# Gated linear attention on one core: chunks of 64 tokens joined in pairs

## The chip, the cores and the metric

The kernel runs on one core of a Trainium2 chip. The metric is device time of one execution in microseconds (us); less is better. The core's engines work side by side, each on its own queue in order: TensorE (PE: products; PEld is its loading of weights), VectorE (DVE), ScalarE (ACT), GpSimd (POOL) and SyncE (SP, which here issues nearly all transfers). TensorE multiplies a stationary operand, of up to 128 rows (the contraction) by 128 columns, with a moving one of up to 512 columns, and adds up in banks of PSUM; all else lies in SBUF.

## The reference

A model of four layers on 256 tokens with 2048 channels: RWKV-7, gated linear attention (GLA), SSD, RWKV-7 again. Each layer norms x, shifts and scales it by vectors made from a condition c with the large matrices `ada_w`, mixes tokens, projects out and adds to x. All numbers are float32. The change concerns the GLA layer: 4 heads, 256 key channels and 512 value channels a head, chunks of C = 64 tokens:

```python
qc = chunks(q * DK ** -0.5, DK); kc = chunks(k, DK); vc = chunks(v, DV)
bcum = jnp.cumsum(chunks(log_alpha, DK), axis=-2)          # log decay, summed within the chunk
b_ref = bcum[..., C // 2 - 1:C // 2, :]
scores = jnp.einsum('nbhik,nbhjk->nbhij', qc * jnp.exp(bcum - b_ref), kc * jnp.exp(b_ref - bcum))
o_intra = jnp.einsum('nbhij,nbhjv->nbhiv', jnp.where(causal, scores, 0.0), vc)
b_last = bcum[..., -1:, :]
q_from_start = qc * jnp.exp(bcum)
k_to_end = kc * jnp.exp(b_last - bcum)
def step(state, inp):
    q_n, k_n, v_n, dec_n = inp                             # dec_n = exp(b_last)
    o_n = jnp.einsum('bhik,bhkv->bhiv', q_n, state)
    state = state * dec_n[:, :, 0, :, None] + jnp.einsum('bhjk,bhjv->bhkv', k_n, v_n)
    return state, o_n
_, o_inter = lax.scan(step, state0, (q_from_start, k_to_end, vc, jnp.exp(b_last)))
o = o_intra + o_inter            # then a norm over each head's values, times silu(g), times w_out
```

## The kernel before

Activations lie channel-major: 16 row tiles of 128 channels by 256 tokens. A projection (`proj`, `jobs`, `prods`) streams its weights from HBM in pieces of 128 by 1024 (`raw`, six slots, issued by SP); ACT rounds a piece to its high part H (L310), DVE takes the rest L (L312), and PE adds up three products for each tile of weights: H with both parts of the activation, L with the first (L365). H and L have three slots each. After each piece `tick` puts in as many pieces of the next layers' `ada_w` as a table says; they use the same six slots. Their products are shared: PE takes some (L275), DVE adds the others one row tile at a time (L281), and PE adds up DVE's sums at the end of a group (L285).

In the GLA layer `gla_decay` makes the summed log decays of all heads. Then `paired` calls `gla_head` for each of four heads, and projects out after every second one. `gla_head` does, in the order of the program: project v token-major (for heads after the first); make the decay factors `qe`, `ke` (relative to the middle of each chunk), `qs` (from the chunk's start), `kn` (to its end) and `dec` (of the whole chunk); project q and k and multiply them into these four tiles (L1121, L1124). Then comes the part of the change:

- scores transposed, a block of 64 by 64 for each of four chunks (L1133), clamped and masked by DVE (L1136, L1138) into `sT`;
- `kn` transposed to tokens by PE (L1145), copied by ACT to `kt` (L1147);
- for each chunk: `sT` with v (L1154), plus, from the second chunk on, `qs` with the state (L1157), copied by ACT to `O` (L1158); then, for all chunks but the last, `kt` with v (L1164), which makes the first state by a copy on ACT (L1166) and every later one on DVE as S x dec + product (L1168).

A chunk's 64 tokens are half of the rows (contraction over tokens) or half of the columns (tokens as output). Behind that come the head's norm (L1175 to L1180), four transposes for each half of the tokens (L1183), the projection of g and the gate (L1192 to L1194).

The order of instructions on each engine's queue is not the program's: a planner takes the whole program, with costs and priorities of its own and the slots of each pool, and lays each engine's instructions in one fixed order; an engine then waits for semaphores in that order. So projection products of later parts lie between the products of the chunks. PSUM has five banks in the pool `b1` that this part draws on, and two in `acc` for projections.

Of the kernel before, what the change touches and what calls it, by code (L numbers as in the profile page):

```python
# [15 lines left out]
P = 128  # L16
# [9 lines left out]
# ---------------------------------------------------------------- parameter columns  # L26
# Every vector over channels lies as [128, n/128]: channel t*128+p at row p, column t.
# [29 lines left out]
# ---------------------------------------------------------------- constants of shapes alone  # L57
# [37 lines left out]
# chunks of a projection's weights so far -> chunks of ada's by then  # L95
PACE = ((0, 120, 316, 484, 620), (0, 96, 240, 288, 320))
# chunks of ada's weights that TensorE takes, of each eight: fewer where VectorE has time to spare
# [5 lines left out]
class Lazy:  # L103
    """A list whose entries are made as they are asked for."""
# [12 lines left out]
class Weights:  # L117
    """A matrix in blocks of row tiles and columns, each contiguous: parts of (first column, columns of a block,
    [block of columns, block of row tiles, 128, row tiles x columns])."""
# [3 lines left out]
    def __call__(self, k0, kn, n0, n):  # L123
        """Row tiles k0.., columns n0.., all in one block: [128, kn, n]."""
        a, cols, ap = [p for p in self.parts if p[0] <= n0][-1]
        kt = ap.shape[3] // cols
        assert n == cols and (n0 - a) % cols == 0 and k0 % kt + kn <= kt
        o = k0 % kt * cols
        return ap[(n0 - a) // cols, k0 // kt][:, o:o + kn * cols].rearrange("p (k n) -> p k n", n=cols)


class Kern:
    def __init__(self, ctx, tc, A, out, layers=(0, 1, 2, 3), final=True):
# [20 lines left out]
        # c, and the first weights that it meets, go ahead of all else  # L154
# [16 lines left out]
    # ------------------------------------------------------------ small helpers  # L171
# [8 lines left out]
    def after(self, later, earlier):  # L180
        """The one instruction of an engine goes behind the other."""
        info = mybir.DependencyInfo(mybir.DependencyClass.NoSync, mybir.DependencyReason.DATA)
        self.tc.add_manual_dep(later.ins, earlier.ins.name, info, reason="the earlier one's users wait")
# [4 lines left out]
    def banks(self, ctx, name, **tags):  # L188
        """Functions that give PSUM banks, one for each tag with its number of banks."""
# [34 lines left out]
    # ------------------------------------------------------------ ada: silu(c) @ ada_w + ada_b  # L224
    def ada_all(self):
        """mod third q (0 shift, 1 scale, 2 gate) of every layer as [128, 16]; yields after each chunk of weights.
        Shift and scale of the first layer come together, four columns at a time."""
# [18 lines left out]
    def norm_gain(self, i, m, a, n):  # L246
        """scale -> (1 + scale) * norm_g"""
# [3 lines left out]
    def ada_quarter(self, n, most=32):  # L251
        """Up to n quarters of the first layer's shift and scale, or so many chunks of them."""
        while self.quarters < n and most:
            next(self.ada_gen)
            most -= 1

    def ada_group(self, i, q, n, m):
        """512 columns of third q, in chunks of two row tiles, shared by TensorE and VectorE (its first by ScalarE). Rows 0, 32, 64, 96 of the bank hold 128 columns each."""
# [46 lines left out]
    # ------------------------------------------------------------ projections  # L305
    def split(self, raw, a, n):
        """The exact parts of raw[:, a:a+n]: rounded to float32r, and the rest."""
# [15 lines left out]
    def proj(self, wv, n0, ncols, xs, evac, k0=0, pad=None, tokens=False):  # L323
        """Transposed product: out^T tile j = W[:, n0+128j ...]^T x^T; xs: tiles [128, 2, 256] (parts of x^T).
        evac(j, ps) gets banks [128, nj, 256] with the out tiles j.. j+nj-1. With tokens, the product itself:
        [128 tokens, two tiles of tokens, 256 columns]."""
# [4 lines left out]
    def jobs(self, wv, jobs, xs, k0=0, banks=()):  # L331
        """Blocks of up to 256 columns, a few row tiles of each in turn: (first column, columns, evac, padded, tokens)."""
# [26 lines left out]
    def prods(self, ps, xt, hi, lo, xc, wc, first, last, tokens=False):  # L359
        """ps += W^T x (or x^T W) by the products of the parts."""  # L360
# [6 lines left out]
    def tick(self):  # L367
        """After each chunk of a projection's weights: as many chunks of ada's as keep ahead of their use."""
# [6 lines left out]
    def parts(self, src, bias=None, pool=None, name="xs", **kw):  # L375
        """[128, 256] float32 (+ bias) -> tile [128, 2, 256]: the rounded part and the rest."""
# [11 lines left out]
    def outproj(self, wv, k0, ys, i, norm=None):  # L388
        """x += gate * (W[k0*128 ...]^T y^T), for one group of row tiles. norm: gives a bank for the sums of squares
        of x, which is final then."""  # L390
# [8 lines left out]
        for n0 in range(0, D, cols):  # L399
# [10 lines left out]
            # the norm's short operations wait for nothing else  # L410
# [5 lines left out]
    # ------------------------------------------------------------ norm  # L416
    def squares(self, ps, t):
        """Adds the squares of row tiles t-3..t of x to rows 0, 32, 64, 96 of ps."""
# [10 lines left out]
    def rms(self):  # L429
        """1 / rms of the first x over channels, on every partition: [128, 256]."""  # L430
# [15 lines left out]
    def inv_rms(self, ps, mul, eps, bank):  # L446
        """(sums * mul + eps) ** -0.5 on every partition: [128, 256]."""
# [20 lines left out]
    def norm_parts(self, i):  # L468
        """h = rms(x) * (1 + scale) + shift as parts, x kept."""
# [23 lines left out]
    # ------------------------------------------------------------ RWKV-7  # L493
# [5 lines left out]
    def _rwkv(self, i, j):  # L499
# [6 lines left out]
        # x becomes x / rms * (1 + scale) * norm_g, what h is but for shift; the token before the first is minus shift  # L506
# [27 lines left out]
        # channel-major in DRAM  # L534
# [13 lines left out]
        # v, and the low-rank inner products  # L548
        lora = {}
        with self.tc.tile_pool(name=f"lp{i}", bufs=1) as lp, ExitStack() as ctx:  # L550
# [13 lines left out]
            if i == self.layers[0]:  # L564
                # as shift and scale come in: a quarter of the channels at a time for as many columns as there are banks
# [43 lines left out]
        with ExitStack() as ctx:  # L609
            rb = ctx.enter_context(self.tc.tile_pool(name=f"rb{i}", bufs=2))  # L610
            self.b1, self.b2, self.b3 = self.banks(ctx, f"pb{i}", b1=2, b2=2, b3=1)
            # states of two heads, block diagonal: [channel of (head, k), tile, head, v]
# [16 lines left out]
        # h is no longer needed: x again  # L629
# [31 lines left out]
    def rwkv_first(self, i, j, un, kps, lora, ra):  # L661
        """Four heads (two channel tiles), all tokens in two chunks of 128: what needs no r and v.
        Leaves A, B, K, P (channel-major) and the inverse of I - L in DRAM.

        Decays are taken relative to the middle of the chunk. B and K carry 2^-40, which the masks give back, so
        that the masked part of a product stays finite. The norm of k k_k is applied to rows of L and U instead."""
# [20 lines left out]
        # decay and in-context learning rate  # L687
# [23 lines left out]
        # squares of k k_k, summed over each head: [token, (head of the tile, chunk, tile)]  # L711
# [11 lines left out]
        # k (1 + (a-1) k_a)  # L723
# [4 lines left out]
        # B = k k_k a / P, A = -k k_k P, K = k2 / P  # L728
# [10 lines left out]
        # L transposed, rows scaled  # L739
# [12 lines left out]
    def gram(self, h, which):  # L752
        """s^T t of head h of the tile for four (s, t, chunk, tile): [token of s, 4, token of t].
        One bank holds one half of the rows only."""
# [8 lines left out]
    def rwkv_second(self, i, j, un, spill, kept, rb, last):  # L763
        """The rest of the four heads, in three steps: what needs no state, the chunks in order, the norm. y before
        the gate goes to DRAM."""
# [16 lines left out]
        # bonus sum(r k r_k) v, on the way to be added to y  # L782
# [17 lines left out]
        def prep(c):  # L800
            """The chunk's B, K, V token-major, and its products with K, masked. V loses its mean over the head, and so
            does all that is linear in it; the group norm takes it off anyway."""
# [25 lines left out]
        # chunks in order  # L828
# [41 lines left out]
        # group norm over the head, token-major  # L870
# [21 lines left out]
    def unit_inverse(self, LT, Lf, rk):  # L892
        """Transposed inverse of I - L for eight 128 x 128 strictly lower L, given transposed (above the diagonal)."""
        nc = self.nc
        C, NB = 128, 8
        # diagonal 16 x 16 blocks, one to a row: (block, matrix) x [s, t]
# [35 lines left out]
        # X, and X^T of the odd blocks, as 16 x 16 blocks of 32 x 32 blocks on the diagonal  # L932
# [19 lines left out]
        # 16 -> 32  # L952
        ps = cols(self.b2(), 16)
        for m in range(8):
            for b in range(4):
                # the odd block's columns, and the 16 after them for rows of the bank that stay unused
# [9 lines left out]
        # 32 -> 64  # L966
# [24 lines left out]
        # 64 -> 128  # L991
# [12 lines left out]
    def rsqrt_tiny(self, s, mul, eps, pool):  # L1004
        """(s * mul + eps) ** -0.5 for a small tile [128, n], by Newton steps from a first guess on the bits."""
# [16 lines left out]
    # ------------------------------------------------------------ gated linear attention  # L1022
# [6 lines left out]
    def _gla(self, i, ctx):  # L1029
# [8 lines left out]
        # log decay of all heads, summed over each chunk: [128, 8, 256], times 16  # L1038
# [6 lines left out]
    def gla_v(self, h, vt):  # L1045
        """Blocks of v, token-major."""
# [5 lines left out]
    def gla_decay(self, win, hs, bc, vt):  # L1052
        """The decays, and the first head's v on the way."""
# [27 lines left out]
    def paired(self, n, part, wout, i):  # L1081
        """Parts of four row tiles each, projected out two at a time once the next part's first products are queued."""
# [9 lines left out]
    def gla_head(self, h, hs, win, bc, due, vt):  # L1092
# [11 lines left out]
        # q, k with their decays  # L1104
# [22 lines left out]
        # scores^T [j, i]: chunk c at rows 64 (c % 2), column block c // 2  # L1127
        HS = (slice(0, 64), slice(64, 128))
        ps = self.b1()
        for c in range(NCH):  # L1130
            hs_, o = HS[c % 2], (c // 2) * C
            for kk in range(2):
                nc.tensor.matmul(ps[hs_, o:o + C], ke[:, kk, c * C:(c + 1) * C], qe[:, kk, c * C:(c + 1) * C],  # L1133
                                 start=(kk == 0), stop=(kk == 1))
# [303 lines left out]
```

## Time and profile before

| what | value |
|---|---|
| median of 3 runs | 2991.27 us (2988.74 to 2991.62) |
| profiled execution, span from first to last instruction | 2990.5 us |
| PE busy | 2870.2 us, 27162 products |
| PEld busy | 2629.9 us |
| DVE busy | 2128.5 us |
| ACT busy | 1402.2 us |
| read from HBM | 620.66 MB, 224 GB/s in and out over the span |

No other time of the profiled execution is listed beside its span. Busy is the time in which at least one instruction of the engine is under way. Products overlap, since each is a pipeline; a product's own duration is thus longer than its distance to the next one, and the chain of waits counts the distance. One float32 product appears as two instructions, a transpose as one. Lines (L1164) are those of the kernel before.

### The profile page before, as it was taken

How to read it: one execution, taken by the hardware profiler on the slowest of the kernel's cores; microseconds unless marked ns; L12 is line 12 of the kernel's file. 1: busy time of each engine (PE TensorE's matmuls, PEld its weight loads, DVE VectorE, ACT ScalarE, POOL GpSimd, SP SyncE). 2: the span in 40 equal slices, each digit the busy share in tenths (PEclk: the TensorE clock that was granted, in tenths of full speed). 3: DMA queues.
4: the chain of work that ended last, by engine and by line, in shares of the span. 5: the costliest groups of instructions: out<-in, count | busy, mean ns of one | idle time of the engine just before them, and what ended most of it. 6: DMA issues, size and time to landing. Idle time of an engine off the chain costs nothing.

```text
span 2990.5 us, 66217 instructions
## 1 busy us (share of the span) xinstructions
PE 2870.2 (96%) x27162; PEld 2629.9 (88%) x27162; DVE 2128.5 (71%) x4008; ACT 1402.2 (47%) x2363; POOL 154.0 (5%) x298
## 2 busy tenths in 40 slices
PE   6899999999999999999999999999889999999997
PEld 4788888899988788988899999999879998999997
DVE  5777885666777756766887687786667888565575
ACT  3474664322336434434555454454457657442233
POOL 0010110101100000000000000000000111010100
PEclk8899999999998999999999999999999999999999
DMA  9877777776675767776776666666556765675543
GB/s 347 313 267 233 250 246 251 293 237 223 203 241 187 233 233 254 261 244 214 253 266 212 231 213 213 214 216 211 162 172 220 228 204 178 211 266 182 168 146 113
DMA packets 239135, 673.82 MB, mean 225 GB/s; under 512 B 72272, under 2 KB 78416, under 8 KB 235760
## 3 DMA queue, kind: packets, MB, share of 16 engines
q1 hardware_dynamic: 217904, 580.84, 58.1%
q0 software_dynamic: 20928, 88.75, 8.2%
q8 instruction: 213, 3.49, 0.5%
q14 instruction: 90, 0.74, 0.1%
HBM read 620.66 MB, written 48.82 MB: 224 GB/s over the span
## 4 chain that ended last, share of the span: by engine, by line
PE 79%; DMA 9%; DVE 6%; issue 3%; SPq 2%; ACT 1%; POOL 0%; DVEq 0%; POOLq 0%; ACTq 0%
PE acc L365 57%; DMA raw<-in_ada_w 4%; PE b L759 3%; PE mx L275 2%; PE pv L365 2%; DVE L L312 2%; DMA raw<-in_rwkv_w_in 1%; DVE adaacc L281 1%; DMA dx<-bd 1%; PE b L868 1%; PE b L1164 1%; PE b L1157 1%; PE b L845 1%; PE b L867 1%; PE b L840 1%
## 5 line engine op out<-in xcount | busy, mean ns | idle before, releaser
L365 PE MATMUL acc<-xs,H 128*128 128x256 f32 x8480 | 1632.0, 290 | 17.9 <-DVE xs L381 7.0
L365 PEld LDWEIGHTS acc<-xs,H 128*128 128x128 f32 x8480 | 1347.3, 194 | 68.7 <-issue 28.2
L365 PE MATMUL acc<-xs,L 128*128 128x256 f32 x4240 | 1223.6, 289 | 3.0 <-DVE L L312 3.0
L310 ACT CAST H<-raw 128x1024 fp32r<-128x1024 f32 (+1 forms) x706 | 718.3, 1018 | 993.7 <-PE acc L365 744.7
L312 DVE TENSOR_TENSOR L<-raw,H 128x1024 fp32r<-128x1024 f32 (+1 forms) x706 | 835.5, 1185 | 374.6 <-ACT H L310 355.8
L365 PEld LDWEIGHTS acc<-xs,L 128*128 128x128 f32 x4240 | 821.6, 194 | 20.9 <-issue 10.4
L281 DVE SCALAR_TENSOR_TENSOR adaacc<-raw,cact,adaacc 128x512 f32<-128x512 f32 x418 | 312.4, 747 | 131.9 <-DMA raw<-in_ada_w 118.3
L365 PE MATMUL acc<-ys,H 128*128 128x256 f32 x1536 | 288.8, 287 | 2.4 <-ACT ys L380 1.4
L365 PEld LDWEIGHTS acc<-ys,H 128*128 128x128 f32 x1536 | 239.9, 191 | 16.6 <-issue 11.9
L365 PE MATMUL acc<-ys,L 128*128 128x256 f32 x768 | 219.1, 286 | 0.0
L365 PEld LDWEIGHTS acc<-ys,L 128*128 128x128 f32 x768 | 146.2, 190 | 4.8 <-issue 4.8
L275 PE MATMUL mx<-raw,cact 128*32 128x128 f32 x2416 | 117.3, 294 | 23.3 <-DMA raw<-in_ada_w 17.5
L403 DVE SCALAR_TENSOR_TENSOR x<-acc,mod,x 128x256 f32<-128x256 f32 x192 | 83.7, 478 | 54.9 <-PE acc L365 54.3
L523 ACT ACTIVATE hn<-x,mod,omu 128x256 f32<-128x256 f32 x192 | 113.2, 599 | 3.1 <-DVE xm L526 1.7
L275 PEld LDWEIGHTS mx<-raw,cact 128*32 128x32 f32 x2416 | 65.2, 114 | 51.2 <-DMA raw<-in_ada_w 15.7
L759 PE MATMUL b<-abkp 64*128 64x128 f32 x768 | 102.7, 288 | 0.2 <-DVE rv L789 0.2
L759 PEld LDWEIGHTS b<-abkp 64*128 64x128 f32 x768 | 85.9, 188 | 13.7 <-issue 4.3
L365 PE MATMUL acc<-H,xs 128*128 128x256 f32 x512 | 97.5, 290 | 0.0
L526 DVE SCALAR_TENSOR_TENSOR xm<-x,par,hn 128x256 f32<-128x256 f32 x192 | 88.4, 478 | 1.4 <-ACT hn L523 0.3
L365 PEld LDWEIGHTS acc<-H,xs 128*128 128x128 f32 x512 | 82.4, 197 | 1.2 <-issue 1.2
L365 PE MATMUL acc<-L,xs 128*128 128x256 f32 x256 | 73.6, 289 | 0.0
L821 DVE TENSOR_TENSOR G<-b,cst 128x512 f32<-128x512 f32 x64 | 43.6, 688 | 37.0 <-PE b L759 36.3
(347 smaller groups left out, 3327.0 us busy)
## 6 DMA issues: line engine op xcount, KB each, us to landing
raw<-in_ada_w SPq DMA_DIRECT2D x384, 512.0 KB, 5.1
raw<-in_rwkv_w_in SPq DMA_DIRECT2D x256, 512.0 KB, 4.9
raw<-in_ssd_w_in SPq DMA_DIRECT2D x128, 512.0 KB, 4.7
raw<-in_gla_w_in SPq DMA_DIRECT2D x96, 512.0 KB, 4.7
raw<-in_ssd_w_out SPq DMA_DIRECT2D x64, 512.0 KB, 4.4
raw<-in_rwkv_w_out SPq DMA_DIRECT2D x48, 512.0 KB, 3.9
abkp<-kd POOLq DMA_DIRECT2D x16, 1024.0 KB, 6.6
raw<-in_gla_w_out SPq DMA_DIRECT2D x32, 512.0 KB, 4.5
```

What stands on the lines that cost most here:

```text
L275: nc.tensor.matmul(ps[32 * e:32 * e + 32, 0:P], self.cact[:, k:k + 1].broadcast_to([P, 32]), raw[:, u, e * P:(e + 1) * P], start=start, st ...
L281: nc.vector.scalar_tensor_tensor(out=acc, in0=raw[:, u, :], scalar=self.cact[:, k:k + 1], in1=acc, op0=ALU.mult, op1=ALU.add)
L310: nc.scalar.copy(out=hi, in_=raw[:, a:a + n])
L312: nc.vector.tensor_tensor(out=lo, in0=raw[:, a:a + n], in1=hi, op=ALU.subtract)
L365: self.nc.tensor.matmul(ps, lhs, rhs, start=first and part == 0 and w is hi, stop=last and w is lo)
L403: nc.vector.scalar_tensor_tensor(out=self.x[:, t, 1:], in0=ps[:, u, :], scalar=gate[:, t:t + 1], in1=self.x[:, t, 1:], op0=ALU.mult, op1=A ...
L523: nc.scalar.activation(t1, x[:, k, 1:], AF.Identity, scale=self.omu[:, col:col + 1], bias=self.mods[(i, 0)][:, k:k + 1])
L526: done[k] = nc.vector.scalar_tensor_tensor(out=xm, in0=x[:, k, 0:T], scalar=self.p("rwkv_mu", col), in1=t1, op0=ALU.mult, op1=ALU.add)
L759: self.nc.tensor.matmul(ps[:, n * C:(n + 1) * C], s[r, q, c * C:(c + 1) * C], t[r, q, c * C:(c + 1) * C], start=True, stop=True)
L821: nc.vector.tensor_tensor(out=G[h].rearrange("p (w q) t -> p w q t", w=2), in0=g.rearrange("p (w q) t -> p w q t", w=2), in1=self.c("kmask ...
L840: nc.tensor.matmul(ps[:, n * H:(n + 1) * H], G[h][:, q, :], tk[:, 2, q, HS[h]], start=not c, stop=not c or h == 1)
L845: nc.tensor.matmul(ps[:, n * H:(n + 1) * H], Tt[:, 4 * h + 2 * c + q, :], Rh[:, n, :], start=True, stop=True)
```

## The change

Two chunks of 64 are treated as one block of 128 tokens. The scores of a pair are a block of 128 by 128, formed of four 64 by 64 blocks: those on the diagonal from `ke` and `qe` as before, those off it from `kn` and `qs`, the one above the diagonal with them, and masked. The scores' product with v is one product of 128 tokens for each pair. The state is formed once, after the first pair, from `kn` of the first chunk scaled by the second chunk's decay and `kn` of the second as it is; it is read once, by the second pair, with `qs` of the fourth chunk scaled by the third's decay. Both scalings are done in place by DVE. The many other hunks of the diff take out comments and docstrings, so that line numbers differ.

```diff
@@ -1124,51 +1124,51 @@
...
         self.proj(win, 1024 + 256 * h, 256, hs, evk)
         HS = (slice(0, 64), slice(64, 128))
         ps = self.b1()
-        for c in range(NCH):
-            hs_, o = HS[c % 2], (c // 2) * C
-            for kk in range(2):
-                nc.tensor.matmul(ps[hs_, o:o + C], ke[:, kk, c * C:(c + 1) * C], qe[:, kk, c * C:(c + 1) * C],
-                                 start=(kk == 0), stop=(kk == 1))
-        sT = gu.tile([P, 2, C], F32, name="sT")
-        nc.vector.tensor_scalar(out=sT.rearrange("p c t -> p (c t)"), in0=ps[:, 0:2 * C], scalar1=3e38, scalar2=-3e38,
+        for s in range(2):
+            for bi in range(2):
+                i = slice((2 * s + bi) * C, (2 * s + bi + 1) * C)
+                for kk in range(2):
+                    for bj in range(2):
+                        j = slice((2 * s + bj) * C, (2 * s + bj + 1) * C)
+                        l, r = (ke, qe) if bi == bj else (kn, qs)
+                        nc.tensor.matmul(ps[HS[bj], s * P + bi * C:s * P + (bi + 1) * C], l[:, kk, j], r[:, kk, i],
+                                         start=(kk == 0), stop=(kk == 1))
+        sT = gu.tile([P, 2, P], F32, name="sT")
+        nc.vector.tensor_scalar(out=sT.rearrange("p c t -> p (c t)"), in0=ps[:, 0:T], scalar1=3e38, scalar2=-3e38,
                                 op0=ALU.min, op1=ALU.max)
-        nc.vector.tensor_tensor(out=sT, in0=sT, in1=self.c("gmask").unsqueeze(1).broadcast_to([P, 2, C]),
+        nc.vector.tensor_tensor(out=sT, in0=sT, in1=self.c("tri128").unsqueeze(1).broadcast_to([P, 2, P]),
                                 op=ALU.mult)
-        kt = gu.tile([P, 2, 2, P], F32, name="kt", bufs=1)
+        d4 = dec.rearrange("p (k c) o -> p k c o", c=NCH)
+        for t, c, o in ((kn, 0, 1), (qs, 3, 2)):
+            t = t[:, :, c * C:(c + 1) * C]
+            nc.vector.tensor_tensor(out=t, in0=t, in1=d4[:, :, o].broadcast_to([P, 2, C]), op=ALU.mult)
+        kt = gu.tile([P, 2, P], F32, name="kt")
         ps = self.b1()
-        for c2 in range(2):
-            for kk in range(2):
-                nc.tensor.transpose(ps[:, (c2 * 2 + kk) * P:(c2 * 2 + kk + 1) * P], kn[:, kk, c2 * P:(c2 + 1) * P],
-                                    self.c("ident"))
-        nc.scalar.copy(out=kt.rearrange("p a b c -> p (a b c)"), in_=ps)
+        for kk in range(2):
+            nc.tensor.transpose(ps[:, kk * P:(kk + 1) * P], kn[:, kk, 0:P], self.c("ident"))
+        nc.scalar.copy(out=kt.rearrange("p a c -> p (a c)"), in_=ps[:, 0:T])
         O = gu.tile([P, 2, 512], F32, name="O", bufs=1)
-        S = None
-        for c in range(NCH):
-            hs_, tt = HS[c % 2], c // 2
+        S = gu.tile([P, 2, 512], F32, name="S")
+        for s in range(2):
             ps = self.b1()
-            nc.tensor.matmul(ps[hs_], sT[hs_, tt, :], vt[hs_, tt, :], start=True, stop=S is None)
-            if S is not None:
+            nc.tensor.matmul(ps, sT[:, s, :], vt[:, s, :], start=True, stop=s == 0)
+            if s:
                 for kk in range(2):
-                    nc.tensor.matmul(ps[hs_], qs[:, kk, c * C:(c + 1) * C], S[:, kk, :], start=False, stop=(kk == 1))
-            nc.scalar.copy(out=O[hs_, tt, :], in_=ps[hs_])
-            if c == NCH - 1:
-                break
-            S2 = gu.tile([P, 2, 512], F32, name="S")
-            for kk in range(2):
-                ps = self.b1()
-                nc.tensor.matmul(ps, kt[hs_, tt, kk, :], vt[hs_, tt, :], start=True, stop=True)
-                if S is None:
-                    nc.scalar.copy(out=S2[:, kk, :], in_=ps)
-                else:
-                    nc.vector.scalar_tensor_tensor(out=S2[:, kk, :], in0=S[:, kk, :], scalar=dec[:, kk * NCH + c, :],
-                                                   in1=ps, op0=ALU.mult, op1=ALU.add)
-            S = S2
+                    nc.tensor.matmul(ps, qs[:, kk, P:], S[:, kk, :], start=False, stop=kk == 1)
+            nc.scalar.copy(out=O[:, s, :], in_=ps)
+            if not s:
+                for kk in range(2):
+                    ps = self.b1()
+                    nc.tensor.matmul(ps, kt[:, kk, :], vt[:, 0, :], start=True, stop=True)
+                    nc.scalar.copy(out=S[:, kk, :], in_=ps)
         var = gu.tile([P, 2], F32, name="var")
...
```

## Rows read from the trace of the kernel before

**Rows 1.** The page: busy time of each engine; the chain's shares by engine.
```profile
PE 2870.2 (96%) x27162; PEld 2629.9 (88%) x27162; DVE 2128.5 (71%) x4008; ACT 1402.2 (47%) x2363; POOL 154.0 (5%) x298
...
PE 79%; DMA 9%; DVE 6%; issue 3%; SPq 2%; ACT 1%; POOL 0%; DVEq 0%; POOLq 0%; ACTq 0%
```

**Rows 2.** Windows: stretch, length, busy us (instructions), granted clock, DMA share, GB/s.
```profile
1050.00:1060.00 10.00, 10.00 (x95) 9.67 (x94) 7.57 (x9) 3.62 (x4) 0.00 (x0) 1.00 0.93 324
...
1190.00:1200.00 10.00, 10.00 (x35) 4.04 (x34) 3.32 (x4) 2.84 (x4) 0.00 (x0) 1.00 0.14 52
964.00:1370.00 406.00, 399.35 (x3124) 334.47 (x3123) 273.20 (x410) 166.98 (x249) 0.00 (x0) 0.99 0.70 240
1370.00:2200.00 830.00, 812.84 (x7069) 770.30 (x7069) 621.52 (x1166) 394.92 (x584) 9.15 (x15) 0.99 0.65 219
2200.00:2960.00 760.00, 745.67 (x7636) 704.47 (x7636) 529.20 (x1044) 381.68 (x692) 72.80 (x140) 0.98 0.60 194
```

**Rows 3.** Waits of PE, 964 to 1370 us: us in total, times, longest.
```profile
PE acc L365 <- DVE L L312: 2.8, 3, 1.7
PE acc L365 <- ACT H L310: 2.1, 1, 2.1
PE mx L275 <- DVE mod L290: 1.1, 1, 1.1
PE acc L365 <- DVE gth L1193: 0.7, 1, 0.7
```

**Rows 4.** Chain of waits, second head: start us, us, engine, line, instructions.
```profile
1077.99 0.57 PE mx L275 x16
...
1081.50 0.66 PE b L1133 x16
1082.16 0.59 PE b L1145 x4
1082.75 3.83 PE acc L365 x32
1086.58 1.00 PE b L1154 x2
1087.58 1.91 PE b L1164 x4
...
1090.49 1.05 PE b L1164 x2
1091.54 1.73 PE acc L365 x13
...
1094.33 1.00 PE b L1157 x2
...
1107.99 12.91 PE acc L365 x106
```

**Rows 5.** Timeline of PE in the SSD layer, at L1328: start us, us.
```profile
1498.91 1.02 PE L1328 MATMUL b<-xd,bk 128*128 128x512 f32 x2
1499.86 0.43 PE L1338 MATMUL b<-M,xc 128*64 128x128 f32 x2
```

**Rows 6.** Chain of waits, the same place.
```profile
1499.07 0.86 PE b L1328 x2
```

**Rows 7.** Groups by line, DVE and ACT, 964 to 1370 us: busy, mean ns, idle before.
```profile
L1168 DVE SCALAR_TENSOR_TENSOR S<-S,dec,b 128x512 f32<-128x512 f32 x16 | 12.0, 747 | 22.7 <-PE b L1164 22.7
L1158 ACT COPY O<-b 64x512 f32<-64x512 f32 x16 | 9.3, 579 | 48.4 <-PE b L1157 44.6 <-PE b L1154 3.8
...
L1166 ACT COPY S<-b 128x512 f32<-128x512 f32 x8 | 4.7, 585 | 2.5 <-PE b L1164 2.5
...
L1147 ACT COPY kt<-b 128x512 f32<-128x512 f32 x4 | 2.3, 577 | 2.1 <-PE b L1145 2.1
...
L1136 DVE TENSOR_SCALAR sT<-b 128x128 f32<-128x128 f32 x4 | 1.2, 288 | 1.3 <-PE b L1133 1.3
```

**Rows 8.** Waits of DVE, 930 to 1390 us: us in total, times, longest.
```profile
DVE adaacc L281 <- DMA raw<-in_ada_w: 26.5, 23, 3.3
```

## The prediction

> **What bounds the kernel now.** I read the page first: TensorE (PE) is busy for 2870.2 of 2990.5 us, and the chain of work that ended last lies on PE for 79% [rows 1]. A busy share is an average over four layers, so I went to the stage of the change with the view of windows: the gated-linear-attention (GLA) layer's heads run from about 964 to 1370 us. PE is busy there for 399.35 of 406 us, that is 6.65 us idle; VectorE (DVE) for 273.20, ScalarE (ACT) for 166.98; the DMA share is 0.70 and the granted clock 0.99 [rows 2], so nearly all of it at the 2.4 GHz level. The view of waits, cut to that stage, names all that PE waited for there: six waits, 6.7 us together, none of them at a line that the diff touches [rows 3]. The chain of waits through the second head shows the same from the other side: from the scores (L1133) to the last product with the state (L1157) every step is a PE step, and each begins where the last one ended [rows 4]. So in this stage time is what PE's queue holds: an instruction taken out of it is time taken out, until another engine or the weights' transfers come late.
>
> **The change part by part, in PE's queue.** One float32 product is two instructions in the trace, a transpose is one. Old cost of a head, from the chain of the second head [rows 4]:
> - scores: 16 instructions, 0.66 us; transposes of k: 4, 0.59 us;
> - sT with V (L1154): 4 products at 1.00 = 4.00 us;
> - q with the state (L1157): 3 chunks by 2 = 6 products at 1.00 = 6.00 us;
> - k with V (L1164): the first two together 1.91, four more at 1.05: 6.11 us.
> Sum 17.36 us, 69.4 us over four heads. (The other three heads have the same steps of the same lengths.)
>
> New cost of a head:
> - Products of 512 columns: 2 + 2 + 2 = 6 instead of 16, now with 128 rows and 128 columns of weights. That shape stands in the trace in the next layer, L1328: it starts at 1498.91 and the next product at 1499.86, so 0.95 us [rows 5]. 6 x 0.95 = 5.70 us. From below: the chain counts 0.86 for it [rows 6]; from above the 1.05 of a lone L1164. I take 0.95 because it is the same shape.
> - Scores: the diff forms all four 64 by 64 blocks of a pair, the masked one too: 32 instructions instead of 16. At 0.66 / 16 = 0.041 us that is 1.32 us. Bounds: 0.57 / 16 = 0.036 (L275, quarter-width weights, [rows 4]) gives 1.14; straight down from 512 columns (1.00 / 2 x 64 / 512 = 0.0625) gives 2.0. I take 0.041, it is the same shape.
> - Transposes: 2 instead of 4, at 0.59 / 4 = 0.147: 0.30 us.
> Sum 7.32 us. Saved: 17.36 - 7.32 = 10.04 us a head, **40.2 us** in four heads. With all lower prices 17.36 - (5.16 + 1.14 + 0.30) = 10.76, or 43.0 us; with all upper ones 17.36 - (6.30 + 2.0 + 0.30) = 8.76, or 35.0 us.
>
> The inner loop of the new scores alternates between the two column halves of the array at each product. The Trainium skill, "TensorE: Matmul & The Clock Gate", Part 3, says that products whose outputs lie at different column groups run side by side. The trace agrees in part, 0.041 against 0.0625 above; by the rule in full the new scores would cost 16 x 0.0625 = 1.0 us, and the saving would be 1.3 us more over the layer. My sum stays at 0.041.
>
> **Gaps around the small products.** Between the chunk products the planner lays projection products (L365). After the transposes, which use the whole array, 32 of them take 3.83 us, 0.120 each; at the end of the stage 106 take 12.91, 0.122 each. Right behind a half-array product 13 take 1.73, which is 0.15 more than 13 x 0.122 [rows 4]. The second head has six such returns (the first and the last are in the rows), so up to 6 x 0.15 x 4 = 3.6 us lie in gaps. The new products use the whole array, but no row shows one of them followed by L365, so I take half: **1.8 us** more saved, bounds 0 and 3.6.
>
> **Other engines.** DVE loses four state updates (0.747 each) and a clamp and mask at 128 columns (0.288, and about the same), 3.56 us a head [rows 7]. It gains clamp and mask at 256 columns, at most twice 0.288 each, and two scalings of 128 columns (estimate 0.288 each, the nearest shape): at most 1.73. So at least 1.8 us less a head. ACT loses two of four O copies (0.579) and part of the k copy (0.577), and keeps the two S copies (0.585): at least 1.16 us less [rows 7]. Neither was the bound, so this is worth nothing by itself. In about 366 us DVE would have 266 of work, 73%. The transfers stay the same in number: 0.70 x 406 = 284 us of DMA time in 366 us is 0.78. Single stretches already run at 0.93 without a wait of PE, while the chunk stages fall to 0.14 [rows 2]: which I read as full weight buffers. It is this slack that the shorter stage eats, about 10 us of some 15 to 20 a head. SBUF slots and PSUM banks of this stage are asked for less often (8 banks a head instead of 14), so I cost them at nothing.
>
> **The new wait.** k and q of one chunk are scaled in place on DVE, behind the scores (which read them unscaled), and the transposes that stood right behind the scores on PE [rows 4] now need that scaling. On DVE it stands behind the clamp, the mask and whatever weight splitting (L312) or ada sum (L281) is queued; an ada sum waits for its transfer up to 3.3 us [rows 8]. Behind the waiting transposes on PE's in-order queue stand projection products, which would wait with them. Against that, the state's chain goes: three rounds of product, update and read become one. Bounds: nothing, if the planner lays enough projection products between (it laid 32, 3.83 us, between the old transposes and L1154), and 3.3 us a head, 13.2 in all. I take one wait of the present mean, 6.7 / 6 = 1.1 us, in two of four heads: **2.2 us**, since PE's waits in this stage now have that size [rows 3].
>
> **Sum.** 40.2 + 1.8 - 2.2 = 39.8 us off the profiled span of 2990.5 us: 2950.7 us. The median of the runs, 2991.27, is 0.8 us above that span; no other time of the profiled execution is listed, so I take 0.8 as what lies around it: **2951.5 us**.
>
> **Rivals.**
> - *DVE's queue holds the transposes.* Every head pays the longest wait, 13.2 us: 2990.5 - 40.2 - 1.8 + 13.2 + 0.8 = 2962.5 us. For it: the scaling is behind four kinds of work on an in-order queue. Against: PE now has no wait at any chunk step, though the old chain crossed to DVE and back twice a head. Chance 0.11.
> - *The halves already ran side by side.* If products of the two chunks of a pair overlapped in different halves of the array, six of the ten products that go (two of each kind) were free, and only four of about 1.0 us count; less 0.36 a head for scores and transposes together, 4 x 3.64 = 14.6 us: 2976.7 us. Against: L1154 and L1164 follow each other at full length, 1.00 and 1.91, then 1.05 [rows 4]; the planner laid no two halves of one kind together. Chance 0.03.
>  The Trainium skill, "TensorEngine Tiling (Array Packing)", Tiling Modes, Key Properties, says that different tiles of the array can run products in parallel, which speaks against merging halves. By that rule this rival would be the forecast; the rows show no overlap between the 512-column products, so it keeps its small chance.
> - *More than forecast.* All gaps go and all products cost the lower price: 43.0 + 3.6 = 46.6 us, 2944.7 us. For it: full-array products among full-array products. Against: L1328 itself shows 0.95. Chance 0.05.
> - *Slower.* The order on the queues is the planner's, and a shorter stage moves its choices in all that follows: SSD and the second RWKV layer. PE is idle there for 830 - 812.84 and 760 - 745.67, 31.5 us together [rows 2]. Should that idle time more than double (from 40 us more on), the gain is gone; if it tripled, 2951.5 + 63 = 3014.5 us. For it: nothing fixes that order. Against: the chunk order of weights and ada transfers is written by program counters and not by time, and those layers' work is not touched. Chance 0.03.
> - That the change doesn't do what it says (work kept) has no room: the loops count 6 products.
>
> **How the numbers follow.** The forecast has 0.78; its own bounds, without rivals, run from 43.0 + 3.6 saved to 35.0 saved with a wait of 2.2: 2944.7 to 2958.5. With the first rival and a little reordering elsewhere the range for 8 in 10 is 2942 to 2964 us; the overlap, the slower case and the tails lie outside. A difference under 0.2% (6 us) can't be told from none with this kernel. Faster: 0.78 + 0.11 + 0.03 + 0.05, less 0.01 that I leave to no difference: 0.96; same 0.01; slower 0.03.
>
> **What would show it.** Right: 48 instead of 128 instructions of 512 float32 columns in the layer, each product about 0.95 us from start to start; scores near 1.3 us a head; the heads' stage near 366 us instead of 406, PE idle in it still under 10 us, DMA share near 0.78; the 830 and 760 us of the two later layers about unchanged. Wrong: PE waiting at the transposes for the scaled k by microseconds a head (first rival); the stage shortened by 40 us but a later layer longer (last rival); products of 1.05 us or more, or scores near 2 us (the upper prices).

## The result and the profile after

The changed kernel takes 2953.75 us (median of 4 runs, 2947.10 to 2968.06) against 2991.44 in the same comparison: a ratio of 0.9877, 95% interval 0.9857 to 0.9898. Measured again, the same two kernels gave 2950.40 against 2990.68: 0.9866, 0.9848 to 0.9885. The forecast was 2951.5 us. The gain is some 38 to 40 us, as the sum had it. Its parts are not: the stage of the change gave more than forecast, and later layers took some of it back.

The page of the changed kernel: busy time of each engine, and the chain's shares by engine. Its span, 2966.2 us, is the longest of the four runs; two more traces of the same kernel (`again`, `again_2`) have 2951.6 and 2941.2.

```profile
PE 2840.5 (96%) x27138; PEld 2637.4 (89%) x27138; DVE 2118.3 (71%) x4000; ACT 1396.5 (47%) x2355; POOL 154.3 (5%) x298
...
PE 77%; DMA 11%; DVE 6%; issue 3%; SPq 2%; ACT 1%; POOL 0%; DVEq 0%; POOLq 0%; ACTq 0%
```

To compare stages I cut both programs at the same products: the first product of the decays (L1067), the SSD layer's first broadcast of its norm (L455), the last L455 ahead of the second RWKV layer, and the last of all. The first stretch begins with PE's first product. The GLA stretch by windows, before and after (columns as in [rows 2]):

```profile
940.20:1426.60 486.40, 472.46 (x3715) 399.10 (x3714) 329.33 (x497) 206.76 (x308) 0.00 (x0) 0.98 0.71 243
```

```profile
949.20:1388.80 439.60, 425.60 (x3691) 391.76 (x3690) 318.73 (x488) 200.23 (x300) 0.00 (x0) 0.99 0.78 268
```

46.8 us are gone from this stretch, and PE's busy time in it is 46.86 us shorter; PE is idle for 14 us in both. The same length of work left PE's queue and the stretch. The heads' stage alone, 406 us before [rows 2] and forecast near 366, takes 359 us, with PE idle for 7.2:

```profile
973.00:1332.00 359.00, 351.78 (x3097) 326.77 (x3097) 262.87 (x401) 159.35 (x239) 0.00 (x0) 1.00 0.79 270
```

The four stretches in all traces, in us (the names of the changed forms are explained with the experiments):

| trace | RWKV 1 | GLA | SSD | RWKV 2 |
|---|---|---|---|---|
| before | 935.2 | 486.4 | 786.9 | 764.7 |
| before_2 | 931.9 | 485.6 | 785.5 | 767.1 |
| before_3 | 935.8 | 485.7 | 787.1 | 766.0 |
| after | 944.2 | 439.6 | 789.2 | 775.6 |
| again | 926.6 | 440.7 | 788.2 | 778.4 |
| again_2 | 928.6 | 438.1 | 787.7 | 769.1 |
| old_side_by_side | 931.5 | 466.1 | 786.7 | 765.7 |
| column_halves | 930.1 | 443.0 | 786.0 | 766.3 |
| pv_halves | 925.3 | 445.1 | 787.6 | 773.9 |
| ten_more | 926.2 | 476.1 | 787.8 | 774.6 |
| no_scaling | 936.4 | 441.9 | 786.5 | 767.7 |
| no_state | 927.2 | 430.5 | 785.2 | 770.2 |
| no_state_2 | 928.5 | 431.5 | 786.9 | 768.7 |
| no_state_halves | 938.8 | 433.0 | 785.9 | 774.4 |

Means of three: GLA 485.9 before and 439.5 after, 46.4 us less; SSD 1.9 more, RWKV 2 8.4 more, RWKV 1 (the same instructions in the same order on every queue) 1.2 less.

The chain of waits through the second head of the changed kernel (L1138 scores, L1154 transposes, L1161 scores with v, L1169 k with v, L1164 q with the state; to be read against [rows 4]):

```profile
1078.81 0.26 PE b L1138 x2
1079.07 0.55 PE acc L365 x3
1079.61 1.08 PE b L1138 x30
1080.69 3.31 PE acc L365 x26
1084.00 0.22 PE b L1154 x2
...
1086.37 0.55 PE mx L275 x10
1086.92 1.05 PE b L1161 x2
1087.98 1.72 PE b L1169 x4
1089.69 0.86 PE b L1161 x2
...
1092.76 1.72 PE b L1164 x4
1094.48 12.58 PE acc L365 x105
```

A product of 512 columns is 0.86 us and 1.05 only as the first behind quarter-width ones (L275); the six are 5.35 us. The chain is still PE's alone: 3.31 us of projection products fill the time in which DVE scales k. PE's waits in the heads' stage (us in total, times, longest), and the new DVE and ACT groups (lines 1141 to 1170):

```profile
PE acc L365 <- DVE L L312: 3.7, 4, 1.7
PE acc L365 <- ACT H L310: 2.5, 2, 2.0
PE acc L365 <- ACT ys L380: 0.5, 1, 0.5
PE acc L365 <- DVE gth L1193: 0.5, 1, 0.5
```

```profile
L1165 ACT COPY O<-b 128x512 f32<-128x512 f32 x8 | 4.7, 585 | 16.6 <-PE b L1164 12.8 <-PE b L1161 3.9
L1170 ACT COPY S<-b 128x512 f32<-128x512 f32 x8 | 4.5, 582 | 1.1 <-PE b L1169 1.0
...
L1143 DVE TENSOR_TENSOR sT<-sT,cst 128x256 f32<-128x256 f32 x4 | 1.7, 420 | 0.0
L1141 DVE TENSOR_SCALAR sT<-b 128x256 f32<-128x256 f32 x4 | 1.7, 418 | 0.0
...
L1155 ACT COPY kt<-b 128x256 f32<-128x256 f32 x4 | 1.5, 367 | 0.7 <-PE b L1154 0.7
L1149 DVE TENSOR_TENSOR kn<-kn,dec 128x128 f32<-128x128 f32 x4 | 1.1, 288 | 0.4 <-PE b L1138 0.4
L1149 DVE TENSOR_TENSOR qs<-qs,dec 128x128 f32<-128x128 f32 x4 | 1.1, 287 | 0.0
```

Eight waits and 7.2 us where six and 6.7 stood [rows 3], none at a transpose or a chunk product.

### The profile page after: what moved, and what is told of

Same layout as the page of the kernel before. It is cut to its first block, busy times and chain, and to the rows that moved or that the text cites. A ratio compares the mean times of both kernels' runs of the same rounds, so it can differ in the third digit from the quotient of the medians.

```text
span 2966.2 us, 66151 instructions
## 1 busy us (share of the span) xinstructions
PE 2840.5 (96%) x27138; PEld 2637.4 (89%) x27138; DVE 2118.3 (71%) x4000; ACT 1396.5 (47%) x2355; POOL 154.3 (5%) x298
## 4 chain that ended last, share of the span: by engine, by line
PE 77%; DMA 11%; DVE 6%; issue 3%; SPq 2%; ACT 1%; POOL 0%; DVEq 0%; POOLq 0%; ACTq 0%
PE acc L365 57%; DMA raw<-in_ada_w 4%; PE b L759 3%; PE mx L275 2%; DMA raw<-in_rwkv_w_in 2%; PE pv L365 2%; DVE L L312 1%; DVE adaacc L281 1%; DMA sp<-yd 1%; PE b L868 1%; PE b L867 1%; PE b L845 1%; DMA xd<-dx 1%; PE b L692 1%; ACT H L310 1%
## 5 line engine op out<-in xcount | busy, mean ns | idle before, releaser
L275 PE MATMUL mx<-raw,cact 128*32 128x128 f32 x2416 | 118.9, 296 | 24.6 <-DMA raw<-in_ada_w 19.9
L275 PEld LDWEIGHTS mx<-raw,cact 128*32 128x32 f32 x2416 | 65.9, 114 | 52.8 <-DMA raw<-in_ada_w 18.7
L526 DVE SCALAR_TENSOR_TENSOR xm<-x,par,hn 128x256 f32<-128x256 f32 x192 | 88.7, 479 | 1.5 <-ACT hn L523 0.3
```

Of the source, the lines that this page charges most:

```text
L275: nc.tensor.matmul(ps[32 * e:32 * e + 32, 0:P], self.cact[:, k:k + 1].broadcast_to([P, 32]), raw[:, u, e * P:(e + 1) * P], start=start, st ...
L526: done[k] = nc.vector.scalar_tensor_tensor(out=xm, in0=x[:, k, 0:T], scalar=self.p("rwkv_mu", col), in1=t1, op0=ALU.mult, op1=ALU.add)
```

## The experiments

Theory A: the stage is what PE's queue holds, so each product taken out or put in counts with its distance on PE (from the end of the one before it to its own end). Rivals: the shorter chain across engines gave the gain; the new wait costs; the old halves overlapped or could have.

**ten_more.** Ten products that nobody reads, behind the two state products:

```diff
+                ps = self.b1()
+                for x in range(10):
+                    nc.tensor.matmul(ps, kt[:, x % 2, :], vt[:, 0, :], start=x == 0, stop=x == 9)
```

> The changed kernel with ten more products of 128 by 128 by 512 columns a head, as many as the change took away, into a PSUM bank that nothing reads; nothing waits for them. Theory A (the stage is what PE's queue holds): 10 x 0.86 x 4 = 34 us longer than the changed kernel, nearly the time of before. Theory B (the change gained by the shorter chain of waits, state updates on VectorE above all, and PE has time to spare): under 17 us longer.

Measured: 2983.43 us against 2950.40 of the changed kernel on the same chip, 33.0 longer; the GLA stretch is 36.6 us longer than the mean of the changed kernel's. The chain of waits, second head:

```profile
1077.17 1.72 PE b L1169 x4
1078.88 8.58 PE b L1173 x20
1087.47 0.86 PE b L1161 x2
```

The ten stand in the chain with 0.858 us each, and 4 x 8.58 = 34.3 us. Theory A holds: nothing in this stage hides a product on PE. With PE idle for 14 us of the stretch before and after, the shorter chain across engines is not what was gained.

**column_halves.** Each of the six products as two of 64 output columns:

```diff
-                    nc.tensor.matmul(ps, kt[:, kk, :], vt[:, 0, :], start=True, stop=True)
+                    for o in HS:
+                        nc.tensor.matmul(ps[o], kt[:, kk, o], vt[:, 0, :], start=True, stop=True)
```

(and likewise for the other two kinds)

> The changed kernel with each of the six 512-column products of a head done as two of 64 output columns, in the two column halves of the array, one right behind the other; same arithmetic. Theory A (products in different halves of the array run one after the other, as the old chain rows read): 12 products of about 1.0 us instead of 6 of 0.86, 6.8 us a head, some 27 us longer than the changed kernel. Rival (they run side by side, and the old halves did too where they were independent): at most 6 x 0.15 us a head, under 4 us longer.

Measured: 2944.74 us, GLA stretch 443.0: not 27 us longer, but 3.5 in the stretch, and in time not longer at all. The chain, second head (L1162 scores with v, L1173 k with v, L1166 q with the state):

```profile
1072.63 1.01 PE b L1162 x4
1073.64 1.72 PE b L1173 x8
1075.35 0.86 PE b L1162 x4
1076.21 0.35 PE mx L275 x6
1076.56 1.74 PE acc L365 x13
1078.30 1.87 PE b L1166 x8
```

Twice the instructions, the same time: four in 0.86 us. Two products with outputs in different halves of the columns do run side by side when they stand next to each other. My reading of the old rows fell here: the halves of [rows 4] cost a full product each because of what stood next to them, not because the array can't overlap them; the next run puts that to the test. The Trainium skill ("TensorEngine Tiling (Array Packing)", Key Properties) states that different tiles of the array can run products in parallel. Here the trace agrees, with 0.86 us for two.

**old_side_by_side.** So the old kernel was tried with its own 16 products in another order (and O copied by ACT once a pair, not once a chunk):

```diff
+            for c in pair:
+                hs_ = HS[c % 2]
+                nc.tensor.matmul(po[hs_], sT[hs_, s, :], vt[hs_, s, :], start=True, stop=c == 0)
+            U = {}
+            for kk in range(2):
+                for c in pair[:2 - s]:
+                    hs_ = HS[c % 2]
+                    U[c, kk] = self.b1()
+                    nc.tensor.matmul(U[c, kk], kt[hs_, s, kk, :], vt[hs_, s, :], start=True, stop=True)
...
             for kk in range(2):
...
+                for c in pair:
+                    if before[c] is not None:
+                        nc.tensor.matmul(po[HS[c % 2]], qs[:, kk, c * C:(c + 1) * C], before[c][:, kk, :],
+                                         start=False, stop=(kk == 1))
+            nc.scalar.copy(out=O[:, s, :], in_=po)
```

> The kernel before with the same products in another order, and O copied once a pair: the two chunks' products with V stand next to each other (different row and column halves of the array), the first four of k with V alternate between the row halves into four banks, and one pair of reads of the state stands together. The number of products, states and reads is that of before. Theory A' (what the change took away were half-array products that happened to stand alone; laid side by side they overlap, as the halves of column_halves did): a head's 16 products cost 2 x 1.0 + 2 x 0.9 + 2 x 0.95 + 5 x 1.0 = 10.7 us instead of 16.1, so some 21 us shorter than before, that is half of what the change brought in its stretch. Theory A (half products follow one another, only fewer products help): within 6 us of before.

Measured: 2969.89 us against 2991.45, ratio 0.9928, 0.9913 to 0.9943; the GLA stretch is 466.1, 19.8 us shorter than before. The chain, second head (L1156 scores with v, L1162 k with v, L1177 q with the state):

```profile
1077.59 1.01 PE b L1156 x4
1078.59 1.92 PE b L1162 x8
1080.51 1.86 PE acc L365 x14
1082.37 1.00 PE b L1177 x2
1083.37 1.01 PE b L1156 x4
1084.38 1.00 PE b L1177 x2
1085.38 1.91 PE b L1162 x4
1087.29 1.00 PE b L1177 x2
...
1090.09 1.01 PE b L1177 x4
1091.09 0.91 PE acc L365 x6
1092.00 1.00 PE b L1177 x2
```

Two products with v, in different rows and columns, take 1.01 us as one did; four of k with v, alternating between row halves, take 1.92, where two took 1.91 [rows 4]. The 16 products cost 10.86 us a head instead of 16.11, 21.0 over four heads. So 20 of the 46 us of the stretch were to be had with the old algorithm, by order alone; the other 26 came with the pairing. Whether a still better order of the old products would give more was not tried.

**no_scaling.** The two DVE scalings left out:

```diff
-            nc.vector.tensor_tensor(out=t, in0=t, in1=d4[:, :, o].broadcast_to([P, 2, C]), op=ALU.mult)
+            pass
```

> The changed kernel without the two in-place scalings of k and q (its output lacks the factors dec there), so that the transposes wait for no new DVE step. My prediction put the new wait at 2.2 us in all, its rival at 13.2. If the planner's projection products cover it, as the trace of the changed kernel reads: within 3 us of the changed kernel, and its GLA stretch 440 us within 2. By the rival: some 10 us shorter.

Measured: 2950.20 us, GLA stretch 441.9. The transposes now stand right behind the scores, and nothing is gained: the new wait cost nothing, and the prediction's first rival is out.

**no_state.** One step further:

```diff
         for kk in range(2):
-            nc.tensor.transpose(ps[:, kk * P:(kk + 1) * P], kn[:, kk, 0:P], self.c("ident"))
-        nc.scalar.copy(out=kt.rearrange("p a c -> p (a c)"), in_=ps[:, 0:T])
+            nc.tensor.matmul(ps[:, 0:P], kn[:, kk, 0:P], qs[:, kk, P:], start=(kk == 0), stop=(kk == 1))
+        nc.scalar.copy(out=sX, in_=ps[:, 0:P])
...
+                nc.tensor.matmul(ps, sX, vt[:, 0, :], start=False, stop=True)
```

> One step further than the change: no state at all. The second pair's part from the first is a score block of 128 by 128 from the scaled k and q (2 products of 128 columns) and one product with v; the transposes, the two state products, the two reads and three ACT copies go. Theory A (PE's queue sets the stage): a head loses 3 products of 0.86 and 0.22 of transposes and gains about 0.44: 2.4 us a head, 9.4 us less than the changed kernel, about 37 to 50 us less than before. Theory B (the chain across engines had set the stage, and the change already took it away): within 3 us of the changed kernel.

Measured: 2936.49 us, ratio to before 0.9828, 0.9810 to 0.9846; the stretch 430.5, 9.0 us shorter than the changed kernel's, where 9.4 was expected. Second head (L1154 the cross block, L1160 the two products of the scores with v, L1162 that of the cross block):

```profile
1064.19 0.44 PE b L1154 x4
...
1066.18 1.91 PE b L1160 x4
1068.09 0.35 PE mx L275 x8
1068.44 1.05 PE b L1162 x2
```

This form is shorter than both kernels, by 9.0 us of its stretch against the changed one. Measured again (theory B', a cost of the planner's order in the later layers, comes up below):

> no_state again, beside no_state_halves on the same chip: 2936 us within 4; a second trace of its second RWKV layer: 770 us or more, PE idle 14 to 17 us by theory B', anything between 764 and 778 by its rival.

Measured: 2937.01 us, 0.9825 (0.9801 to 0.9848).

**Where the rest went.** The stretch is 46.4 us shorter and the time only 38 to 40. The first question was the spread of single runs, with two more traces of the changed kernel:

> The changed kernel once more, for a second trace. In its first trace the stretch from the decay products (L1067) to the SSD layer's first L455 was 46.9 us shorter than before, but the first RWKV layer, where the order of instructions is the same as before, was 9.1 us longer, SSD 2.3 and the second RWKV layer 10.9. Theory A (those 22 us are the spread of single runs): the GLA stretch is again 442 us within 2, and the first RWKV layer comes out nearer to 908 than to 917 us; the second RWKV layer moves too. Theory B (the planner's new order in SSD and at the start of the second RWKV layer costs it): the second RWKV layer is again 775 us within 2, whatever the first does.

> The changed kernel for a third trace. Spread of single runs: the second RWKV layer below 775 us in this one, or the first at another length than 926.6 and 944.2; the GLA stretch again 440 us within 2. A cost of the new order: the second RWKV layer 775 to 779 us for the third time.

Measured: the GLA stretch 440.7 and 438.1; RWKV 1 926.6 and 928.6; RWKV 2 778.4 and 769.1. (The 908 and 917 us of the first expectation are the start of that layer's first L455; in `again` it is 900.2.) The first layer runs the same instructions in the same order in all 14 traces and spreads from 925.3 to 944.2 us. A good part of that is the clock: in single runs a stretch of work gets the lower of TensorE's two levels (1.2 GHz, a granted clock of 0.50). By the granted clock of the traces the layer has 116.1 us at that level in its longest one and 85.3 to 88.7 in the five shortest. Most of the rest is PE's idle time, 55.3 to 66.4 us: `old_side_by_side` has least of the lower level (75.1) and most idle time, and lies in the middle. The lower level is seen in RWKV 2 of `again` too, 2815 to 2835 us:

```profile
2815.00:2825.00 10.00, 10.00 (x44) 8.92 (x43) 5.07 (x10) 0.98 (x3) 0.33 (x1) 0.54 0.33 105
2825.00:2835.00 10.00, 10.00 (x46) 9.55 (x46) 4.74 (x11) 2.50 (x4) 0.00 (x0) 0.50 0.16 54
```

PE is busy throughout, but with half the instructions that it does at 2.4 GHz: the granted clock is 0.50. Just ahead of it PE had been idle for 1.95 us at L788 (waiting for DVE). The third trace of the kernel has no such stretch there, though PE idles for 1.44 us in these 10 us too:

```profile
2815.00:2825.00 10.00, 8.56 (x68) 7.88 (x68) 8.56 (x16) 3.48 (x7) 0.00 (x0) 1.00 0.21 65
```

For RWKV 2 that alone did not close the question, since the trace of the kernel before was short there:

> The kernel before once more, for a second trace of it. If the second RWKV layer's 764.7 us in its first trace was one draw of a spread (clock at the lower level in some stretches of single runs), it comes out elsewhere between 764 and 778 us now, and the GLA stretch again at 486 us within 2. If the new order costs the changed kernel there: again 765 us within 2.

> The kernel before for a third trace. Ten traces of changed kernels, with either order of the later layers, have 766 to 778 us in the second RWKV layer, mean 772; the two of the kernel before have 764.7 and 767.1. If the kernel before draws from the same spread, a value over 769 us comes about two times in three; if the changed kernels pay some 6 us there by something other than the order, it is again 764 to 768 us.

Measured: 767.1 and 766.0, the GLA stretch 485.6 and 485.7. With the old algorithm (four traces, old_side_by_side among them) the layer takes 764.7 to 767.1, with PE idle for 10.7 to 11.3 us (worked out from the products' starts and durations, without the 3.0 us ahead of the last product); in ten traces of the pairing it takes 766.3 to 778.4, mean 771.9, PE idle 11.1 to 17.0. A planner's order that costs was the obvious theory: the changed kernel's order in SSD and at the start of RWKV 2 differs from before, while column_halves has the old order there and was short. Two kernels were made to restore that order by splitting one kind of product: no_state_halves, shown here against no_state, and pv_halves, which splits the changed kernel's two products of the scores with v in the same way:

```diff
-                nc.tensor.matmul(ps, sX, vt[:, 0, :], start=False, stop=True)
+                for o in HS:
+                    nc.tensor.matmul(ps[o], sX[:, o], vt[:, 0, :], start=False, stop=True)
```

> no_state with its one product of the cross block with v done in two column halves side by side. In the stage that costs nothing worth counting (0 to 0.15 us a head), but with it the planner's order of the SSD and the second RWKV layer is that of the kernel before again, as it was in column_halves and old_side_by_side, and not that of the changed kernel. Theory B' (the new order in the later layers costs about 8 us: 1 in SSD, 6 to 7 in the second RWKV layer, where PE idles 15 to 17 us instead of 11): about 8 us shorter than no_state in these rounds, some 2928 us, the second RWKV layer 764 to 768 us, PE idle in it 11. Rival (only the spread of single runs): within 3 us of no_state.

> The changed kernel with only the two products of the scores with v done in column halves; the later layers' order is again that of the kernel before. Theory B': 7 to 9 us shorter than the changed kernel, 2942 to 2945 us, as column_halves was; the GLA stretch 440 us within 3. Rival: 2950 us within 3.

Measured: no_state_halves 2943.38 us (0.9839, 0.9816 to 0.9862), RWKV 2 774.4, PE idle 16.0. That is 6.4 us longer than no_state_2, which neither theory had. It is also no test of the order, since the traces show no_state itself with the old order of RWKV 2 on PE, DVE and ACT; no_state_2 takes 768.7 there, PE idle 11.7. The test is pv_halves against the changed kernel: 2950.30 (0.9863, 0.9846 to 0.9880), RWKV 2 773.9, PE idle 16.6, in the old order (its GLA stretch, 445.1, is above the 440 within 3 that was expected). That theory fell: five traces of the pairing in exactly the old order of RWKV 2 take 766.3 to 774.4, five in the new one 767.7 to 778.4.

What the time is made of can be read from the traces. Take from the length of RWKV 2 all of PE's idle time (here with the 3.0 us) and half of the time in which PE was busy at the lower level, since it gets through about half of its products there (the rows above): 739.4 to 741.0 us are left in each of the 14 traces, while the lengths spread over 14 us. The same sum leaves 831.6 to 835.0 us of the first layer. So the work of these layers is nearly the same everywhere. Of the 6.0 us that the ten traces of the pairing are longer on average than the four others, 4.1 are PE's idle time and 1.5 the clock; of the 8.4 us of the changed kernel's three traces, 5.0 and 3.5. Why PE waits more in most kernels with pairing stays open: single runs of one kernel differ in this layer by 9 us, and four traces against ten do not show a mechanism.

## Why the prediction was right, and where it was not

- *PE's queue bounds the stage.* Right: busy time and stretch shrank by the same 46.8 us, and ten products put back cost 0.858 us each.
- *40.2 us for the instructions.* Slightly small. Per head: products 5.70 forecast, 5.35 in the second head (0.86 each, 1.05 for the first); scores 1.32, measured 0.26 + 1.08 = 1.34 (the 1.0 us of full overlap between the column halves did not come); transposes 0.30, measured 0.22. That is 6.91 against 7.32, and 4 x (17.36 - 6.91) = 41.8 us. Over all four heads, by the products' ends, it is 69.6 - 27.3 = 42.3 us; the 1.05 stands only in the second. The mis-sized term is the product: 0.95 was L1328's distance to the start of a product of another width; between products of its own width the 0.86 of [rows 6] counts, the lower bound.
- *1.8 us for gaps.* About right, as far as it can be read. The stretch is 46.4 us shorter in the mean, 4.1 more than the instructions, but not all of that is gaps: PE is idle for 0.6 us less, and busy at the lower clock level for 7.8 us instead of 11.2 (means of three), which is worth about 1.7. So 1.8 is left; pairs of traces with the same time at the lower level (before_2 and again, before_3 and after) leave 2.2 and 2.6. Behind the new products 105 projection products take 12.58 us, 0.120 each with no excess; the six returns of the second head are gone. No run of its own shows the gaps alone.
- *2.2 us for the new wait.* Nothing of it came: no PE wait at the transposes, and no_scaling is no faster. The planner laid 26 projection products in front of the transposes.
- *Other engines cost nothing.* Right; clamp and mask are 0.418 and 0.420 us instead of the 0.576 that bounded them, and the DMA share of the heads' stage rose from 0.70 to 0.79, against 0.78 worked out.
- *The halves' rival, 0.03.* Right that the 512-column halves did not overlap in the old order, wrong in the step that took this for a property of the products: "L1154 and L1164 follow each other at full length". They do where the next one differs in kind. The rule of the Trainium skill that I set aside ("TensorEngine Tiling (Array Packing)", Key Properties) is what column_halves and old_side_by_side show, with two products in 0.86 and 1.01 us. It changes no time of this comparison, but it changes what the change is: 20 of its 46 us undo an unlucky order.
- *The later layers "about unchanged".* Wrong for RWKV 2 in part: 8.4 us longer in the mean of three traces, and SSD 1.9. The stage gave 6.6 us more than the 39.8 of the sum: 2.1 from the instructions, 2.2 from the wait that did not come, and some 2.3 from idle time and clock, which differ between runs. The later layers took that and a little more. So the mechanism of the stage was right, and that the total came out at the forecast is luck: two misses of 6.6 and some 10 us that nearly cancel.

## What to carry to other kernels

Where PE is busy throughout, count its queue by the distances in the chain of waits, and take a product's price between neighbours of its own shape. Before merging half-size products, try them next to each other in different halves of the array: here that gave 20 us for a change of order. Judge a change of 1% by the stretch it touches, cut at the same instructions in several traces; layers that run the same instructions differed by up to 19 us between single runs. Before reading a cause into such a difference, take out PE's idle time and half of its busy time at the lower clock level.

## What the runs showed of the hardware that was not expected

Two float32 products of 512 columns in different column halves, or in different row halves into different banks, took together what one takes (0.86 to 1.01 us for two; 1.92 for four). A half-size product between products of other shapes took 1.00 to 1.05, more than a whole one among its like (0.86). Stretches of several us at the lower clock level, with PE busy in them, come and go between runs of the same program: 17.5 us of them in the second RWKV layer of `again_2`, 37.9 in that of `again`.
